# Products accumulated chunk by chunk beside the modulation loads, the modulation spread over heads and merge, and the last FFN weights kept on chip

## The chip, the cores and the metric

One Trainium2 chip; the program runs on all 8 of its cores. Each core does one batch element of the same layer, and the cores exchange nothing. The metric is device time in microseconds (us) of the slowest core. Some executions fall into a slower state: the cores of one die, or of both, show a lower granted TensorE clock than the others, and the time is longer.

## The reference, cut to what matters

```python
cond = jax.nn.silu(c)                                   # c: (8, 2048)
mod = (cond @ w_ada[l] + b_ada[l])[:, None, :]          # 2048 -> 6*2048: shift, scale, gate, twice
sh1, sc1, gt1, sh2, sc2, gt2 = jnp.split(mod, 6, axis=-1)
h = rmsnorm(x, norm1_w[l]) * (1.0 + sc1) + sh1          # x: (8, 2048 tokens, 2048)
x = x + gt1 * hybrid_mixer(h, ...)     # h @ w_in; 8 A heads and 4 B heads; gated merge; @ w_o
h = rmsnorm(x, norm2_w[l]) * (1.0 + sc2) + sh2
x = x + gt2 * swiglu(h, w_ffn_in[l], w_ffn_out[l])      # hidden width 5632
return rmsnorm(x, final_norm_w)
```

All inputs are float32. `w_ada` alone is 96 chunks of 128 output columns, 1 MB each in float32, used once per batch element. The first 32 (shift and scale of the first norm) are needed before the first product of the mixer. The other 64 are needed later: the first gate in the projection, shift and scale of the second norm before the FFN, the second gate in the FFN's output.

## The kernel before: the parts that matter

The kernel works through the 2048 tokens in two halves of 1024. Each half has the stages heads (projections and recurrences of the 12 heads), merge, projection and FFN. Before the first half there is a start stage: load x, compute the norm, form 32 modulation chunks. Every operation goes into a graph. A list scheduler with a rough time model picks, for each engine, the order in which the operations are emitted: among ready operations, the lowest key first. So the order on an engine is fixed when the program is built.

```python
    def schedule(self):                        # (cut)
            for o in cand[e]:
                if o.ready <= bt + 1e-9:
                    k = o.key
                    ...
                    if pk is None or k < pk:
                        pick, pk = o, k
```

Weights come through a ring of slots of 4 KB per partition, by loads that GpSimd (POOL) issues and that cast float32 to bf16. Everything that is loaded with `wload` shares this ring, and loads are issued in one order.

```python
        def wload(src, ncols, key=0.0):
            i = wpos[0] % NSLOT                # NSLOT = 7
            wpos[0] += 1
            t = sb(WOF + i * 4096, ncols, BF16)
            ...
            dma('pool', t, src, wsem[i], writes=[full], nbytes=128 * ncols * 4, key=key - 20.0)
            return t

        def ada_chunk(m, w, cond):             # one modulation chunk: a 2048-column product-sum on VectorE (DVE)
            stt(w, w, 1.0, cond, ALU.mult, ALU.mult, accum=col(modr, m), key=2.0)
```

The start, with a ring of five modulation chunks of its own:

```python
        def phaseA_first():
            adar = ring(172 * KB, 5, 2048, BF16)
            for k in range(16):                # x, in 16 loads of 128 x 1024 float32, from another queue (SP)
                dma('sp', xall[k], xT[k, :, 0:ST], xsem[k], writes=[xall[k]], nbytes=1 << 19, key=-500)
            for i in range(32):
                kc, m = i // 2, (16 if i % 2 == 0 else 0) + i // 2
                w = adar()
                dma('pool', w, w_ada_d[m], asem[i % 5], writes=[w], nbytes=1 << 20, key=-400)
                ada_chunk(m, w, cond0)
                ...                            # squares of x, their sum, the norm
                        for hf in range(2):    # 32 multiplies by the norm, keys 0 to 1.5: ahead of the products' 2.0
                            tt(H(xall[k], hf), H(xall[k], hf), H(rs, hf), ALU.mult, key=0.1 * k)
            for k in range(16):                # then h, on ScalarE (ACT)
                for hf in range(2):
                    act(H(hT[k], hf), H(xall[k], hf), AF.Identity, bias=col(mod, k), scale=col(a1, k), key=0.1 * k)
```

The other 64 chunks, in the first half: two per step of merge, projection and first FFN quarter, through the weight ring.

```python
                dense(w_in_d[72 + fc], hT, ev_mb)      # merge
                if s == 0:
                    ada_some(2, condC)                 # wload + ada_chunk + small columns
            ...
            for fc in range(12):
                proj(fc, (0, 1), wload(w_o_d[fc], 2048))
                if s == 0:
                    ada_some(2, condC)
```

The end of each half normalises and stores in two halves of 512 tokens (`final(0)`, `final(1)`), each 16 tiles.

Of the kernel before, what the change touches and what calls it, by code (L numbers as in the profile page):

```python
# [7 lines left out]
F32 = mybir.dt.float32  # L8
# [11 lines left out]
NSLOT = 7  # L20
# [56 lines left out]
class Graph:  # L77
# [15 lines left out]
    def op(self, eng, fns, reads=(), writes=(), cost=0.2, key=0.0, dsem=None, nbytes=0, table=None):  # L93
# [11 lines left out]
        for t in writes:  # L105
            for k in t.keys:
                w = self.lastw.get(k)
                if w is not None:
                    preds.setdefault(w, 1)
                for r in self.readers.get(k, ()):  # L110
                    preds.setdefault(r, 1)
        preds.pop(o.idx, None)
# [120 lines left out]
def build_nc(trace=None):  # L233
# [21 lines left out]
    with ExitStack() as es:  # L255
# [108 lines left out]
        def act(out, in_, func, bias=None, scale=None, key=0.0):  # L364
# [8 lines left out]
            g.op('act', lambda e: e.activation(out=out.ap, in_=in_.ap, func=func, **kw), reads=[in_] + aps,  # L373
                 writes=[out], cost=cost, key=key, table=TABLE.get(func))

        def tt(out, in0, in1, op, key=0.0, in1ap=None, outap=None, in0ap=None):
# [3 lines left out]
                 reads=[in0, in1], writes=[out], cost=0.155 + in0.ncols * 0.00104, key=key)  # L380

# [7 lines left out]
        def stt(out, in0, s, in1, op0, op1, key=0.0, accum=None):  # L389
# [3 lines left out]
            g.op('dve', lambda e: e.scalar_tensor_tensor(out=out.ap, in0=in0.ap, scalar=v, in1=in1.ap, op0=op0, op1=op1, **kw),  # L393
# [13 lines left out]
        def dma(q, out, in_, sem, reads=(), writes=(), nbytes=0, key=0.0):  # L407
            oa = out.ap if hasattr(out, 'keys') else out
            ia = in_.ap if hasattr(in_, 'keys') else in_
            g.op(q, lambda e: e.dma_start(out=oa, in_=ia), reads=list(reads), writes=list(writes), dsem=sem,  # L410
                 nbytes=nbytes, cost=0.6, key=key)
# [6 lines left out]

        def wload(src, ncols, key=0.0):
            i = wpos[0] % NSLOT  # L420
            wpos[0] += 1
            t = sb(WOF + i * 4096, ncols, BF16)
            full = sb(WOF + i * 4096, 2048, BF16)
            dma('pool', t, src, wsem[i], writes=[full], nbytes=128 * ncols * 4, key=key - 20.0)
            return t

        def H(t, hf):
            return t.cols(hf * 512, hf * 512 + 512)

        def dense_half(w, acts, hf, evac, gk=GK):  # L430

            nk = len(acts)
            p = bank(dbank())
            for k0 in range(0, nk, gk):
# [3 lines left out]
                mm(fns, [w] + [H(acts[k], hf) for k in ks], [p], 0.2154 * len(ks))  # L438
                g.K += 0.2154 * len(ks)
# [9 lines left out]
        osem = [g.newsem("o") for _ in range(16)]  # L449
        csem = [g.newsem("c") for _ in range(10)]  # L450
        cond_f = sb(200 * KB - 8 * KB, 2048, F32)

        def load_cond(dst, tmp, sem):
            dma('sp', tmp, c_d[0:1, :].broadcast_to([128, D]), sem, writes=[tmp], nbytes=1 << 20)
            act(dst, tmp, AF.Silu)

        dma('sp', smalls, smalls_d[:, :], csem[0], writes=[smalls], nbytes=1 << 16)
        cond0 = sb(200 * KB, 2048, BF16)
        load_cond(cond0, cond_f, csem[1])
        for t_, c0, s_ in ((ident, 0, 2), (m64, 128, 3), (m128, 640, 4), (cm64, 1152, 5), (cm128, 1664, 6)):  # L460
            dma('pool', t_, cst_d[:, c0:c0 + t_.ncols], csem[s_], writes=[t_], nbytes=t_.ncols * 512)
# [20 lines left out]
        def ada_chunk(m, w, cond):  # L482
            stt(w, w, 1.0, cond, ALU.mult, ALU.mult, accum=col(modr, m), key=2.0)


        def norm_finish(acc, rs, hf):
            p = bank(sbank())
# [5 lines left out]
        def phaseA_first():  # L493
            adar = ring(172 * KB, 5, 2048, BF16)
            asem = [g.newsem("a") for _ in range(5)]
            xall = [sb(Y + 4 * KB * k, 1024, F32) for k in range(16)]
            acc = sb(MG, 1024, F32)
            rs = sb(MG + 4 * KB, 1024, F32)
            r_q = ring(MG + 8 * KB, 3, 1024, F32)
            for k in range(16):  # L500
                dma('sp', xall[k], xT[k, :, 0:ST], xsem[k], writes=[xall[k]], nbytes=1 << 19, key=-500)
            for i in range(32):
                kc, m = i // 2, (16 if i % 2 == 0 else 0) + i // 2
                w = adar()
                dma('pool', w, w_ada_d[m], asem[i % 5], writes=[w], nbytes=1 << 20, key=-400)
                ada_chunk(m, w, cond0)
                if i % 2 == 0:
                    ts(col(a1, kc), col(modr, m), col(bsc1, kc), sm(SM_N1 + kc), ALU.add, ALU.mult)
                else:
                    tt(col(mod, m), col(modr, m), sm(SM_BADA + m), ALU.add)  # L510
                if i < 16:
                    q = r_q() if i else acc
                    act(q, xall[i], AF.Square, key=-300)
                    if i:
                        tt(acc, acc, q, ALU.add, key=-300)
                if i == 15:
                    for hf in range(2):
                        norm_finish(acc, rs, hf)
                    for k in range(16):
                        for hf in range(2):  # L520
                            tt(H(xall[k], hf), H(xall[k], hf), H(rs, hf), ALU.mult, key=0.1 * k)
            for k in range(16):
                for hf in range(2):
                    act(H(hT[k], hf), H(xall[k], hf), AF.Identity, bias=col(mod, k), scale=col(a1, k), key=0.1 * k)


        def phaseA_next(s, step):
            tok0 = s * ST
            if step < 16:
# [6 lines left out]
                dma('sp', x, xT[k, :, tok0:tok0 + ST], xsem[k % 2], writes=[x], nbytes=1 << 19)  # L536
# [12 lines left out]
            for hf in range(2):  # L549
# [4 lines left out]
                if k < 12:  # L554
                    dma('sp', x, xT[k, :, tok0 + hf * 512: tok0 + hf * 512 + 512], xsem[2 + (k % 2) * 2 + hf], writes=[x], nbytes=1 << 18)
# [55 lines left out]
        def frontA(i, h):  # L611
# [20 lines left out]
            dense(w_in_d[8 + i], hT, ev_f)  # L632
            dense(w_in_d[i], hT, ev_q)
            dense(w_in_d[24 + i], hT, ev_g)

        def gk_low():
            dma('sp', wgk2, wgk2_d[:, :], csem[7], writes=[wgk2], nbytes=1 << 18, key=-30)
            dma('pool', wgkl, wgkl_d[:, :], csem[8], writes=[wgkl], nbytes=1 << 18, key=-30)
# [122 lines left out]
        def ada_some(n, cond):  # L761
            for _ in range(n):
                if ada_todo:
                    m = ada_todo.pop(0)
                    ada_chunk(m, wload(w_ada_d[m], 2048), cond)
                    blk = m // 16
                    tt(col(mod, m), col(modr, m), sm(SM_BADA + m), ALU.add, key=2.0)
                    if blk == 2:
                        ts(col(gt1h, m - 32), col(mod, m), 0.5, None, ALU.mult, ALU.bypass, key=2.0)
                    if blk == 4:  # L770
                        ts(col(a2, m - 64), col(mod, m), 1.0, sm(SM_N2 + m - 64), ALU.add, ALU.mult, key=2.0)

        phaseA_first()
        for s in range(NST):
            tok0 = s * ST

            vt = None
            for i in range(8):
                h = newhead(1)
                frontA(i, h)  # L780
                if i % 4 == 0:
                    vt = vgroup(i // 4)
                tail(h, 64, 128, vt, (i % 4) * 128, persA[i], SM_ANW, [yT[i]])
            gk_low()
            for i in range(4):
# [4 lines left out]
                tail(h, 128, 256, vt, (i % 2) * 256, persB[i], SM_BNW, [yT[8 + 2 * i], yT[9 + 2 * i]])  # L790

# [5 lines left out]
            condC = sb(196 * KB, 2048, BF16)  # L797
            if s == 0:
                load_cond(condC, sb(Z, 2048, F32), csem[0])
                ada_todo += list(range(32, 48)) + list(range(64, 80)) + list(range(48, 64))  # L800
            cst = {}

            def merge_a(fc):
# [17 lines left out]
                if s == 0:  # L821
                    ada_some(2, condC)
# [43 lines left out]
            for fc in range(12):  # L866
# [173 lines left out]
```

## Time and profile before

| | us |
|---|---|
| before, timed executions | 3867.65 and 3868.89 fast; 4132.95 and 4259.19 slow |
| before, profiled execution | 3866.53, fast |
| core 5, the slowest: span | 3865.5 |

The page of the profiled execution, in parts: busy time per engine (PE is TensorE, DVE VectorE, ACT ScalarE, POOL GpSimd), then strips of 40 equal slices in tenths busy, then the chain of work that ended last.

```profile
PE 3623.2 (94%) x17656; PEld 1661.3 (43%) x17656; DVE 1432.2 (37%) x2303; ACT 890.1 (23%) x1252; POOL 358.6 (9%) x683
...
PE   0199999999899999999999999999999999999997
...
DMA  8944446878969644565447334555564454544544
...
PE 90%; DMA 5%; DVE 2%; issue 1%; SPq 1%; ACT 0%; POOL 0%; DVEq 0%; ACTq 0%; POOLq 0%
```

TensorE is on the chain for 90% of the span, and its strip shows where it is not busy: the first two slices (a slice is 97 us), one dip at the eleventh, the end. In all views L393 and the like are lines of the kernel's source, often those of a helper; SB is the on-chip memory, PS the accumulators that matmuls write. The next view gives the busy time of each engine in chosen stretches of core 5. The columns after the bounds are the stretch's length, busy time and number of instructions of PE, PE's weight loads, DVE, ACT and POOL, then the granted TensorE clock, the mean busy share of the 16 DMA engines, and the rate in GB/s.

```profile
core 5: us, PE busy (x) PEld busy (x) DVE busy (x) ACT busy (x) POOL busy (x), PEclk, DMA share, GB/s
0.00:97.00 97.00, 3.66 (x4) 1.18 (x4) 36.43 (x61) 24.99 (x25) 9.84 (x22) 0.93 0.82 174
97.00:197.00 100.00, 17.10 (x49) 6.05 (x50) 83.45 (x105) 23.89 (x32) 14.24 (x27) 0.59 0.89 142
217.00:623.00 406.00, 405.94 (x2351) 195.64 (x2349) 210.39 (x427) 199.96 (x270) 27.44 (x52) 1.00 0.41 68
...
963.00:1178.00 215.00, 188.77 (x829) 82.67 (x828) 126.21 (x179) 58.33 (x83) 26.39 (x50) 0.94 0.84 146
1178.00:2020.00 842.00, 842.00 (x3898) 381.69 (x3897) 219.60 (x303) 112.85 (x168) 77.57 (x147) 1.00 0.57 101
3836.00:3866.00 30.00, 2.96 (x7) 0.69 (x4) 22.14 (x34) 2.48 (x4) 0.00 (x0) 0.60 0.72 269
```

In 1178:2020 PE is never idle: 3898 matmuls in 842 us are 0.216 us each. The Trainium skill ("TensorE: Matmul & The Clock Gate", Part 1) gives 215.7 ns from start to start for a matmul of 512 columns once warm; the trace agrees. So a stage can be judged by how long it takes for its number of matmuls. In the first 197 us there are 48 dense ones. The heads (217:623) have no PE gap, and DVE and DMA are only half and two fifths busy there: that is the room which the change wants to use.

The start in time order. The first line is the DMA strip of 0 to 200 us in slices of 5 us; then come lines of the timeline of DVE, POOL and PE (start, duration, instruction, count, and in brackets the idle time before it and what ended that).

```profile
DMA  3999999999999997200008999999999999999920
```

```profile
82.19 19.35 DVE L377 TENSOR_TENSOR SB<-SB 128x512 f32<-128x512 f32 x32 [4.52 <-ACT SB L373]
101.46 2.28 DVE L393 SCALAR_TENSOR_TENSOR SB<-SB 128x2048 bf16<-128x2048 bf16 x1
...
104.30 0.53 POOL L410 DMA_DIRECT2D SB<-w_ada_l  x1 [93.09 <-DVE SB L393]
...
121.56 5.24 PE L436 MATMUL PS<-SB 128*128 128x512 bf16 x16 [40.84 <-ACT SB L373]
```

The five chunks of the ring fill early. DVE gets to the first one at 101.5 us, after all 32 multiplies. Only then can POOL issue the sixth chunk (104.30, after 93 us), and in the strip the DMA engines stand from about 80 to 105 us. The tail: DVE first runs the 16 outputs of the previous 512 tokens (10.7 us), and only then reaches the last evacuations, the norm and 16 more.

```profile
3833.45 10.69 DVE L393 SCALAR_TENSOR_TENSOR SB<-SB 128x512 f32<-128x512 f32 x16 [0.43 <-ACT SB L373]
...
3848.58 2.04 PE L488 MATMUL PS<-SB 128*128 128x512 f32 x2 [11.67 <-DVE SB L377]
...
3852.14 10.69 DVE L393 SCALAR_TENSOR_TENSOR SB<-SB 128x512 f32<-128x512 f32 x16 [3.71 <-ACT SB L373]
```

### The profile page before, as it was taken

What the parts mean: (1) busy time and instruction counts of PE and PEld (TensorE: products, weight loads), DVE (VectorE), ACT (ScalarE), POOL (GpSimd) and SP (SyncE); (2) the same over time, 40 slices, a digit from 0 to 9 for tenths busy, and PEclk for the clock granted to TensorE, in tenths of its full rate; (3) what the DMA queues carried; (4) which work ended last, traced back from release to release, by engine and by line L of the source; (5) the groups of instructions that cost most, each with busy time, mean ns of one, the idle gap of its engine ahead of it and who ended that gap; (6) DMA issues with size and microseconds to landing.
All of it is one profiled execution on the core that took longest, in us unless ns stands there. A gap on an engine that the chain in (4) does not pass through costs nothing.

```text
span 3865.5 us, 45674 instructions; the slowest of 8 cores (3851.0 to 3865.5 us)
## 1 busy us (share of the span) xinstructions
PE 3623.2 (94%) x17656; PEld 1661.3 (43%) x17656; DVE 1432.2 (37%) x2303; ACT 890.1 (23%) x1252; POOL 358.6 (9%) x683
## 2 busy tenths in 40 slices
PE   0199999999899999999999999999999999999997
PEld 0044444444344444444444444444444444444443
DVE  3845644444653302132145664312143121211116
ACT  2256533111141100030025663311114000000002
POOL 1100000111101100000000000011000000100000
PEclk9599999999899999999999999999999999999998
DMA  8944446878969644565447334555564454544544
GB/s 175 147 71 67 66 67 120 139 128 130 188 107 166 139 77 66 85 137 99 72 71 168 63 58 66 114 77 77 81 126 72 66 86 72 82 77 67 86 68 118
DMA packets 123045, 380.86 MB, mean 99 GB/s; under 512 B 13776, under 2 KB 16720, under 8 KB 122448
## 3 DMA queue, kind: packets, MB, share of 16 engines
q0 software_dynamic: 97776, 315.44, 50.7%
q1 hardware_dynamic: 25056, 62.49, 5.6%
q8 instruction: 145, 2.38, 0.2%
q14 instruction: 68, 0.56, 0.0%
HBM read 676.48 MB, written 16.78 MB: 179 GB/s over the span
## 4 chain that ended last, share of the span: by engine, by line
PE 90%; DMA 5%; DVE 2%; issue 1%; SPq 1%; ACT 0%; POOL 0%; DVEq 0%; ACTq 0%; POOLq 0%
PE PS L436 82%; PE PS L602 5%; DMA SB<-w_ada_l 3%; DVE SB L393 1%; DMA SB<-smalls 1%; SPq L410 1%; DVE SB L377 1%; DMA SB<-w_o_l 1%; DMA SB<-w_in_l 0%; PE PS L712 0%; PE PS L734 0%; PE PS L729 0%; PE PS L651 0%; PE PS L745 0%; DMA SB<-w_fi_l 0%
## 5 line engine op out<-in xcount | busy, mean ns | idle before, releaser
L436 PE MATMUL PS<-SB 128*128 128x512 bf16 x15104 | 3303.4, 381 | 132.3 <-ACT SB L373 105.4
L436 PEld LDWEIGHTS PS<-SB 128*128 128x128 bf16 x15104 | 1477.3, 98 | 1920.9 <-issue 174.7
L373 ACT ACTIVATE SB<-PS 128x512 f32<-128x512 f32 (+1 forms) x580 | 350.2, 614 | 2236.4 <-PE PS L436 2025.1
L377 DVE TENSOR_TENSOR SB<-PS,SB 128x512 bf16<-128x512 f32 x240 | 165.6, 690 | 1041.4 <-PE PS L436 927.5
L373 ACT ACTIVATE SB<-SB 128x512 f32<-128x512 f32 (+5 forms) x504 | 342.4, 713 | 568.3 <-DVE SB L393 276.1
L393 DVE SCALAR_TENSOR_TENSOR SB<-PS,SB 128x512 f32<-128x512 f32 (+1 forms) x400 | 297.0, 747 | 449.0 <-PE PS L436 385.0
L377 DVE TENSOR_TENSOR SB<-SB 128x512 f32<-128x512 f32 (+5 forms) x543 | 333.6, 631 | 220.0 <-ACT SB L373 156.3
L393 DVE SCALAR_TENSOR_TENSOR SB<-SB,PS 128x128 f32<-128x128 f32 (+2 forms) x448 | 206.5, 461 | 406.7 <-PE PS L436 360.7
L393 DVE SCALAR_TENSOR_TENSOR SB<-SB 128x2048 bf16<-128x2048 bf16 (+2 forms) x224 | 307.8, 1398 | 113.5 <-DMA SB<-w_ada_l 92.7
L602 PE MATMUL PS<-SB 128*128 128x512 bf16 x1024 | 232.4, 381 | 6.2 <-DVE SB L401 5.9
L373 ACT ACT_TABLE_LOAD x152 | 195.0, 1283 | 132.2 <-PE PS L436 71.5
L410 POOL DMA_DIRECT2D SB<-w_fi_l x176 | 92.9, 528 | 1018.7 <-PE PS L436 988.3
L602 PEld LDWEIGHTS PS<-SB 128*128 128x128 bf16 x1024 | 98.3, 98 | 120.8 <-issue 9.9
L410 POOL DMA_DIRECT2D SB<-w_in_l x144 | 76.0, 529 | 785.3 <-PE PS L436 421.3
L410 POOL DMA_DIRECT2D SB<-w_fo_l x128 | 67.6, 528 | 637.5 <-PE PS L436 637.5
L488 PE MATMUL PS<-SB 128*128 128x512 f32 x24 | 14.9, 722 | 88.7 <-DVE SB L386 77.1
L410 POOL DMA_DIRECT2D SB<-w_ada_l x96 | 50.8, 530 | 379.3 <-DVE SB L393 158.5
L401 DVE CAST SB<-PS 128x512 bf16<-128x512 f32 x64 | 44.2, 690 | 97.2 <-PE PS L602 97.2
L573 DVE TENSOR_TENSOR_SCAN SB<-SB 128x512 f32<-128x512 bf16 x48 | 58.1, 1218 | 30.1 <-ACT SB L373 30.0
L488 PEld LDWEIGHTS PS<-SB 128*128 128x128 f32 x24 | 4.9, 222 | 92.5 <-issue 91.6
L401 DVE CAST SB<-SB 128x512 bf16<-128x512 f32 x96 | 40.3, 420 | 0.0
L410 POOL DMA_DIRECT2D SB<-w_v_l x32 | 17.0, 544 | 192.6 <-PE PS L436 150.7
(31 smaller groups left out, 373.7 us busy)
## 6 DMA issues: line engine op xcount, KB each, us to landing
SB<-w_fi_l POOLq DMA_DIRECT2D x176, 512.0 KB, 5.2
SB<-w_in_l POOLq DMA_DIRECT2D x144, 512.0 KB, 6.5
SB<-w_ada_l POOLq DMA_DIRECT2D x96, 512.0 KB, 10.1
SB<-w_fo_l POOLq DMA_DIRECT2D x128, 352.0 KB, 4.3
SB<-xT SPq DMA_DIRECT2D x64, 512.0 KB, 12.2
SB<-w_v_l POOLq DMA_DIRECT2D x32, 512.0 KB, 6.2
SB<-w_o_l POOLq DMA_DIRECT2D x32, 512.0 KB, 11.6
outT<-SB SPq DMA_DIRECT2D x64, 256.0 KB, 6.5
```

The lines of the kernel that those rows point to most:

```text
L373: g.op('act', lambda e: e.activation(out=out.ap, in_=in_.ap, func=func, **kw), reads=[in_] + aps, writes=[out], cost=cost, key=key, table= ...
L377: g.op('dve', lambda e: e.tensor_tensor(out=outap if outap is not None else out.ap, in0=in0ap if in0ap is not None else in0.ap, in1=in1ap ...
L393: g.op('dve', lambda e: e.scalar_tensor_tensor(out=out.ap, in0=in0.ap, scalar=v, in1=in1.ap, op0=op0, op1=op1, **kw), reads=[in0, in1] + a ...
L401: g.op('dve', lambda e: e.tensor_copy(out=outap if outap is not None else out.ap, in_=inap if inap is not None else in_.ap), reads=[in_], ...
L410: g.op(q, lambda e: e.dma_start(out=oa, in_=ia), reads=list(reads), writes=list(writes), dsem=sem, nbytes=nbytes, cost=0.6, key=key)
L436: fns = [(lambda e, k=k: e.matmul(p.ap, w.ap[:, k * 128:(k + 1) * 128], H(acts[k], hf).ap, start=(k == 0), stop=(k == nk - 1))) for k in ks]
L488: mm([lambda e: e.matmul(p.ap, onesD.ap, H(acc, hf).ap, start=True, stop=True)], [onesD, H(acc, hf)], [p], 0.9)
L573: g.op('dve', lambda e: e.tensor_tensor_scan(out=dst.ap, data0=mask.ap, data1=src.ap, initial=0.0, op0=ALU.mult, op1=ALU.add), reads=[mask ...
L602: fns = [(lambda e, i=i, j=j, p=p, tb=tb: e.matmul(p.ap, hT[4 * i + j].ap[:, tb * 128:(tb + 1) * 128], ws[i].ap[:, j * 512:(j + 1) * 512], ...
```

## The change

Its intent: let the start's matmuls run while the modulation chunks still come in, put the remaining 64 chunks where DVE and DMA have room, and shorten the end. The diff, cut to its core:

```diff
-NSLOT = 7
+NSLOT = 6
...
-        def phaseA_first():
-            adar = ring(172 * KB, 5, 2048, BF16)
+        def phaseA_first(ws):
+            adar = ring(172 * KB, 8, 2048, BF16)
...
+            for hf in range(2):
+                for k in range(16):                       # x in 32 pieces, first 512 tokens first
+                    x = H(xall[k], hf)
+                    dma('sp', x, xT[k, :, hf * 512:hf * 512 + 512], (xsem, osem[2])[hf][k], writes=[x], nbytes=1 << 18, key=-500)
...                                                         # squares summed on PE instead of DVE
+            banks = [[bank(2 * j + hf) for hf in range(2)] for j in range(4)]
+            hts = []
+            for kc in range(16):
+                for i in range(2):
...
+                    dma('pool', w, w_ada_d[m], asem[n % 8], writes=[w], nbytes=1 << 20, key=-400 + n)
+                    ada_chunk(m, w, -400)
...
+                for hf in range(2):
+                    x = H(xall[kc], hf)
+                    tt(x, x, H(rs, hf), ALU.mult, key=-350)     # now after the products
+                for hf in range(2):
+                    hts.append(act(H(hT[kc], hf), H(xall[kc], hf), AF.Identity, bias=col(mod, kc), scale=col(a1, kc), key=-350))
+                for j in range(4):                              # 4 weights x 2 x 512 tokens = 8 banks
                     for hf in range(2):
+                        p = banks[j][hf]
+                        mm([... ws[j] chunk kc, hT[kc], start=(kc == 0), stop=(kc == 15) ...], key=-100)
...
+        ws = [wload(w_in_d[c_], 2048, key=-380 + 8 * j + 3) for j, c_ in enumerate((8, 0, 24, 9))]
+        banks, hts = phaseA_first(ws)
...
+                if s == 0 and i > 1:
+                    ada_some(3)                           # A heads 2 to 7
...
+                if s == 0:
+                    ada_some(4)                           # B heads
...
-                    ada_some(2, condC)                    # merge keeps 2 per step
+                    ada_some(2)
...
-            for fc in range(12):
+            for fc in range(10):
                 proj(fc, (0, 1), wload(w_o_d[fc], 2048))
-                if s == 0:
-                    ada_some(2, condC)
```

Beside this core, c reaches the 128 partitions through PE instead of by a load of 1 MB; the constants are loaded late; six instead of four products bridge the norm before the FFN; in the last quarter of the FFN all 16 output weights are loaded at once, so that the last 512 tokens can be done as two pieces of 256; and the outputs of `final` get a later key and, for these pieces, stores grouped by four.

## The prediction

> I predict the fast state: the profiled run before took 3866.5 us, the timed runs 3868 to 4259; the slower ones I take for the slow state.
>
> **What bounds it now.** TensorE: the chain of waits is 90% PE. Undisturbed, a dense 128x512 matmul costs 0.216 us (windows, 1178:2020, 3898 matmuls in 842 us). All 17656 at such rates need about 3590 us (estimate), so some 275 us are lost. Matmul counts window by window show where:
> - 0 to 197 us: only 48 dense matmuls (10 us of work); 186 us lost. Timeline: x lands until 73 us; DVE runs 32 normalising multiplies (19 us, ending 101.5) before any modulation product, so the ring of 5 chunks is full and the DMA share falls to 0.1 at 80 to 97. Then 27 chunks come at about 3.2 us each at DMA share 1.0 (11.6 MB in 69 us).
> - 640 to 675 (heads to merge): 9 us, behind a 1 MB broadcast of c.
> - 963 to 1178 (projection and FFN start, first half): 34 us, waits for w_o, w_fi and w_ada, DMA share 1.01, clock 0.82.
> - 2020 to 2072 (between the halves): 8 us.
> - Tail: 28 us from the last dense matmul to the end; DVE first ran 16 outputs of the previous half (10.7 us), then the last evacuations, the norm, and 16 more.
>
> **What the change does, costed.**
> 1. Start. Multiplies now rank after the products, ring 8, constants and c broadcasts leave, four w_in loads join. DMA work: x 8.4 MB at 285 GB/s (hardware queue: 62.5 MB in 5.6% of the span) 30 us; 36 loads at 3.2 us 115; constants 3, two prefetches 6, start-up 3: the last chunk lands near 157 and is used by 164. DVE needs 16 x 5.9 us, so it just hides. By then 128 dense matmuls (27.6 us) are done, against 48 at 197, less 3 us for evacuating eight banks. Gain 47 us. The Trainium skill ("PSUM — Partial Sum Buffer", Specifications) gives eight banks per partition; the start takes them all, so the next products wait for evacuation.
> 2. Modulation: 64 chunks move from merge, projection and FFN into heads and merge. Heads have DMA share 0.42 and DVE at 0.52; 34 chunks of 2.3 us plus small columns add some 90 us of DVE over 440 (to about 0.72) and 0.25 of DMA. Projection then has 16 loads plus x, under the PE's 110 us. Gain 33 + 7, minus 7 us for DVE delays in the heads.
> 3. Six products instead of four hide the norm before the FFN: 1 us.
> 4. Late final outputs at the boundary: 3 us.
> 5. Tail: deferred outputs, last quarter of 256 columns, grouped stores: 28 to about 15 us, less 2 for DVE backlog: 11 us.
> 6. Six weight slots instead of seven: nothing; a slot lasts PE 6.9 us, a load takes 3.2.
>
> Sum about 95 us.
>
> **Prediction: 3770 us, 8 in 10 between 3715 and 3830. Faster by over 2%: 0.69; within 2%: 0.29; slower: 0.02.**
>
> **What would show it.** Windows: dense work steady from 160 to 170 us, DMA share near 1 until then; no PE gap near 640 and in the projection; heads up to 10 us longer, DVE share near 0.7; last matmul to end 13 to 17 us.
>
> **What would make it wrong.** The in-order DVE puts a multiply that waits for the norm ahead of landed chunks, and the DMA idles again (start 185 to 200; time near 3800). The products delay the heads' state chain or hold weight slots and starve PE (20 to 40 us). Or DMA streams overlap better than I add them (3735). Few fast runs.

## The result and the profile after

| | before | after |
|---|---|---|
| fast executions | 3867.65, 3868.89 | 3805.62, 3807.78, 3810.40 |
| slow executions | 4132.95, 4259.19 | 3922.97 (profiled), 4195.23, 4208.56 |
| ratio of fast runs, 95% interval | | 0.9844, 0.9815 to 0.9873: within 2% |

A ratio is the mean time of one kernel's fast runs over the mean of the other's fast runs of the same rounds, so it is not quite the ratio of medians. The output is correct. About 60 us were gained where 95 were predicted; the time lies inside the predicted range, and the class does not match the favoured one.

The profiled execution of the changed kernel was slow, so its cores have to be looked at first. The view of cores:

```profile
core 5: 3801.5 us, clock 0.992
...
die 0 (median of its cores): 3909.1 us, clock 0.958
die 1 (median of its cores): 3792.4 us, clock 0.992
```

Die 1 is undisturbed: its four cores took 3782 to 3805 us, like the cores of the fast executions (3778 to 3810). I therefore read core 5, the same core as before, whose records are complete in both traces. The stretches of core 5 after the change, same columns:

```profile
core 5: us, PE busy (x) PEld busy (x) DVE busy (x) ACT busy (x) POOL busy (x), PEclk, DMA share, GB/s
0.00:97.00 97.00, 46.03 (x46) 12.02 (x46) 25.65 (x50) 18.26 (x29) 10.93 (x24) 1.00 0.98 186
97.00:181.00 84.00, 54.49 (x157) 19.30 (x158) 74.14 (x102) 34.70 (x51) 14.04 (x27) 0.82 0.78 133
181.00:611.00 430.00, 412.79 (x2371) 197.45 (x2369) 303.60 (x579) 221.79 (x292) 47.27 (x90) 0.99 0.68 112
...
954.00:1066.00 112.00, 112.00 (x517) 50.62 (x516) 52.28 (x77) 32.76 (x50) 8.44 (x16) 1.00 0.58 111
1066.00:1981.00 915.00, 915.00 (x4232) 414.67 (x4231) 230.34 (x323) 139.58 (x206) 79.15 (x150) 1.00 0.53 93
3786.00:3802.00 16.00, 0.67 (x2) 0.30 (x2) 7.75 (x19) 2.36 (x6) 2.12 (x3) 0.66 0.39 132
```

The projection (954:1066) and the FFN (1066:1981) are now without a PE gap. The heads (181:611) take 430 us for the work that took 406, and 17 us of PE idling are new there; the other 7 us are in PE's own busy time (413 against 406 us, at a granted clock of 0.99 against 1.00). DVE's 304 us of 430 are 0.71 of the stretch, as predicted.

For a table by stage I count dense 128x512 matmuls along the trace. A stage ends when the first matmul of the next one starts: the first head products, made in the start after the change, are the first 128; the heads end after 1792, merge after 3328, projection after 3840, FFN after 8064.

| stage of core 5, us | before | after | change | predicted |
|---|---|---|---|---|
| start, up to 128 dense matmuls | 216.7 | 180.6 | -36.1 | -47 |
| heads, first half | 406.6 | 430.7 | +24.1 | +7 |
| merge, first half | 346.4 | 342.7 | -3.7 | -7 |
| projection and FFN, first half | 1062.0 | 1026.8 | -35.2 | -34 |
| heads, second half, with the boundary | 444.1 | 441.7 | -2.4 | -3 |
| merge and projection, second half | 446.9 | 446.9 | 0 | 0 |
| FFN, second half, and tail | 942.9 | 932.1 | -10.8 | -11 |
| sum | 3865.5 | 3801.5 | -64.1 | -95 |

(The rows are rounded, so that a sum can be off in its last digit.) The shortfall of 31 us is in the first three rows: 11 in the start, 17 in the heads, 3 in the merge. The rest is as predicted.

The start after the change: first the DMA strip of 0 to 200 us, then DVE.

```profile
DMA  4999999999999999998875525999999995927999
```

```profile
48.99 2.29 DVE L398 SCALAR_TENSOR_TENSOR SB<-SB 128x2048 bf16<-128x2048 bf16 x1 [1.75 <-DMA SB<-w_ada_l]
...
51.40 0.16 DVE L378 TENSOR_TENSOR SB<-SB 128x1 f32<-128x1 f32 x1
94.68 3.10 DVE L378 TENSOR_TENSOR SB<-SB 128x512 f32<-128x512 f32 x5 [43.13 <-ACT SB L374]
```

And POOL, which issues the loads, then PE at the end of the start:

```profile
51.83 0.53 POOL L415 DMA_DIRECT2D SB<-w_ada_l  x1 [3.91 <-DVE SB L378]
100.53 0.53 POOL L415 DMA_DIRECT2D SB<-w_ada_l  x1 [48.17 <-DVE SB L398]
```

```profile
180.56 13.97 PE L449 MATMUL PS<-SB 128*128 128x512 bf16 x64 [0.83 <-ACT SB L374]
```

DVE has done eight products by 51.4 us. The next thing in its order is a multiply by the norm, and it waits for that for 43 us, until ACT has the norm of the first 512 tokens at 94.7. Meanwhile the eight buffers of the ring fill up again, and POOL issues nothing from 51.83 to 100.53. In the strip the DMA engines stay nearly full until about 100 us, because x is still coming in (its last packet landed at 104 us by the trace's DMA records), and then there is a hole: the slices from 100 to 125 us show 7, 5, 5, 2 and 5 tenths, and over these 25 us the mean DMA share is 0.54, so some 12 us of DMA time are empty. From 94.7 on DVE works through 24 products and 32 multiplies until 176.5. Its waits between 95 and 177 us (total us, times, longest; the first wait of 43 us, which ends at 94.7, is counted in):

```profile
DVE SB L378 <- ACT SB L374: 48.0, 2, 43.1
```

So there is one more pause of 4.9 us, for ACT, and none for a modulation chunk: the chain of waits runs through x and the norm of the second 512 tokens to 116.6 us, and from there through DVE's own work to the end of the start. The hole in the DMA strip is not on it.

In the heads, POOL's issues between 286 and 325 us, and PE a little later:

```profile
298.96 0.53 POOL L415 DMA_DIRECT2D SB<-w_ada_l  x1 [3.70 <-DVE SB L398]
303.80 0.53 POOL L415 DMA_DIRECT2D SB<-w_ada_l  x1 [4.32 <-DVE SB L398]
...
322.88 0.53 POOL L415 DMA_DIRECT2D SB<-w_ada_l  x1 [3.01 <-PE PS L632]
323.75 0.53 POOL L415 DMA_DIRECT2D SB<-w_in_l  x1 [0.34 <-issue]
```

```profile
333.90 3.32 PE L449 MATMUL PS<-SB 128*128 128x512 bf16 x8 [2.93 <-DMA SB<-w_in_l]
```

Eight modulation loads in a row are issued between 286.85 and 322.88, five of them after a wait for DVE to finish with the slot's previous chunk. The `w_in` load behind them is issued at once when its turn comes (its own wait is none, "issue"): it had waited only for the loads ahead of it. It lands 10.0 us later, and PE has been idle for 2.9 us by then. The Trainium skill ("DMA: Bandwidth & Descriptors", Anatomy of one DMA) states that a semaphore wait of a load is served on the issuing sequencer, before the load is dispatched; this is what these lines look like. PE's waits on core 5, from 181 to 960 us (total us, times, longest):

```profile
PE PS L449 <- DMA SB<-w_in_l: 8.6, 5, 2.9
PE PS L728 <- DVE SB L398: 4.0, 3, 1.8
PE PS L762 <- DVE SB L406: 2.4, 1, 2.4
PE PS L449 <- DMA SB<-w_upa_l: 2.1, 1, 2.1
```

So there are two sorts of wait: for weights, and for DVE in the heads' state chain (L728 and L762 are its small matmuls). The sizes differ between cores: on core 7, whose heads took 422.9 us, the waits for `w_in` are 0.9 us. After the start, where the prediction charged 3 us for emptying the eight banks, PE's only wait up to 194 us is the 0.83 us for ACT in the line at 180.56.

The tail after the change, by the timeline:

```profile
3789.87 0.67 PE L506 MATMUL PS<-SB 128*128 128x256 f32 x2 [3.96 <-DVE SB L378]
...
3791.64 6.42 DVE L398 SCALAR_TENSOR_TENSOR SB<-SB 128x256 f32<-128x256 f32 x16 [1.91 <-ACT SB L374]
```

The last dense matmul ends at 3785.9, 15.6 us before the end; 13 to 17 had been predicted. No outputs of an earlier piece stand ahead of the last norm any more. No run undoes the boundary, the tail or the six products alone; that they gained what they were meant to is read from the stages only.

### The profile page after: what moved, and what is told of

It reads as the page before. It is cut to its first block, busy times and chain, and to the rows that moved or that the text cites. A ratio compares the mean times of both kernels' runs of the same rounds, so it can differ in the third digit from the quotient of the medians.

```text
span 3921.8 us, 46040 instructions; the slowest of 8 cores (3781.8 to 3921.8 us)
## 1 busy us (share of the span) xinstructions
PE 3776.9 (96%) x17555; PEld 1723.3 (44%) x17902; DVE 1404.3 (36%) x2310; ACT 893.2 (23%) x1287; POOL 379.7 (10%) x709
## 4 chain that ended last, share of the span: by engine, by line
PE 89%; DMA 4%; DVE 2%; SPq 2%; issue 2%; ACT 0%; POOL 0%; DVEq 0%; POOLq 0%; ACTq 0%
PE PS L449 81%; PE PS L632 5%; DVE SB L398 2%; SPq L415 2%; DMA SB<-w_in_l 2%; DMA SB<-w_ada_l 1%; DMA SB<-xT 1%; DMA SB<-w_v_l 1%; PE PS L745 0%; DMA outT<-SB 0%; PE PS L762 0%; PE PS L767 0%; PE PS L778 0%; ACT SB L374 0%; PE PS L506 0%
## 5 line engine op out<-in xcount | busy, mean ns | idle before, releaser
L449 PE MATMUL PS<-SB 128*128 128x512 bf16 (+1 forms) x14837 | 3357.6, 387 | 35.4 <-DMA SB<-w_in_l 12.8
L449 PEld LDWEIGHTS PS<-SB 128*128 128x128 bf16 x15152 | 1508.5, 100 | 1849.8 <-issue 409.4
L374 ACT ACTIVATE SB<-PS 128x512 f32<-128x512 f32 (+2 forms) x585 | 352.1, 613 | 2348.5 <-PE PS L449 2101.9
L398 DVE SCALAR_TENSOR_TENSOR SB<-PS,SB 128x512 f32<-128x512 f32 (+2 forms) x416 | 300.1, 727 | 488.2 <-PE PS L449 438.5
L378 DVE TENSOR_TENSOR SB<-SB 128x512 f32<-128x512 f32 (+6 forms) x517 | 307.5, 610 | 228.5 <-ACT SB L374 161.4
L398 DVE SCALAR_TENSOR_TENSOR SB<-SB 128x2048 bf16<-128x2048 bf16 (+3 forms) x240 | 312.4, 1324 | 72.6 <-DMA SB<-w_ada_l 60.1
L632 PE MATMUL PS<-SB 128*128 128x512 bf16 x996 | 229.1, 381 | 9.0 <-ACT SB L374 6.0
L632 PEld LDWEIGHTS PS<-SB 128*128 128x128 bf16 x1024 | 98.3, 98 | 122.2 <-issue 10.8
L526 PE MATMUL PS<-SB 128*128 128x512 f32 x64 | 52.5, 941 | 45.1 <-ACT SB L374 45.1
L551 PE MATMUL PS<-SB 128*128 128x512 bf16 x125 | 41.5, 488 | 30.5 <-ACT SB L374 30.2
L526 PEld LDWEIGHTS PS<-SB 128*128 128x128 f32 x64 | 14.9, 270 | 81.2 <-issue 80.8
```

Source lines behind the costliest of these rows:

```text
L374: return g.op('act', lambda e: e.activation(out=out.ap, in_=in_.ap, func=func, **kw), reads=[in_] + aps, writes=[out], cost=cost, key=key, ...
L378: g.op('dve', lambda e: e.tensor_tensor(out=outap if outap is not None else out.ap, in0=in0ap if in0ap is not None else in0.ap, in1=in1ap ...
L398: return g.op('dve', lambda e: e.scalar_tensor_tensor(out=out.ap, in0=in0.ap, scalar=v, in1=in1.ap, op0=op0, op1=op1, **kw), reads=[in0, i ...
L449: fns = [(lambda e, k=k: e.matmul(p.ap, w.ap[:, k * 128:(k + 1) * 128], H(acts[k], hf).ap, start=(k == 0), stop=(k == nk - 1))) for k in ks]
L526: mm([lambda e, k=k, hf=hf, q=q: e.matmul(nb[hf].ap, onesD.ap, q.ap, start=(k == 0), stop=(k == 15))], [onesD, q], [nb[hf]], 0.87, key=-300)
L551: mm([lambda e, p=p, j=j, hf=hf: e.matmul(p.ap, ws[j].ap[:, kc * 128:(kc + 1) * 128], H(hT[kc], hf).ap, start=(kc == 0), stop=(kc == 15)) ...
```

## The experiments

Two losses had to be explained. For the start: theory A, DVE's order is at fault (a multiply that waits for the norm stands ahead of landed chunks); theory B, the norm is late because x shares the DMA engines with the weight loads. For the heads: theory C, the products' time on DVE delays the state chain; its rival, the loads of the modulation chunks hold slots of the weight ring and turns of its queue. Twelve kernels were run, each edit made to the changed kernel. Each was timed against the kernel before in the same rounds. Fast runs of the kernel before differ by 0.6% over the chips used (3856 to 3878), so small differences between kernels are read from stages, on cores with complete records, and from the ratios.

### e_order: every multiply tied behind a product that is already in

```diff
-                    tt(x, x, H(rs, hf), ALU.mult, key=-350)
+                late = prods[min(29, 15 + kc)]
+                    tt(x, x, H(rs, hf), ALU.mult, key=-405, after=[late])
```

> One edit to the changed kernel: in the start, the two normalising multiplies of input chunk k are tied behind modulation product 15+k, so the in-order DVE no longer stands for the norm (it stood from 51.4 to 94.7 us) with landed modulation chunks unread. Theory A (DVE order): modulation loads go on while x lands; DMA share stays near 1 and the last first-product matmul group ends near 160 us instead of 177 to 180; total 12 to 20 us less than the changed kernel, ratio to before about 0.980. Rival B (the start is bound by the sum of DMA work, or by x arriving late, whatever the DVE order): x only lands later by what the modulation loads take, and the start still ends at 175 to 185; ratio stays 0.984. The heads should keep their 16 to 23 us of PE gaps in both.

Measured: correct; fast runs 3821.2 and 3824.2. The start took 194 to 198 us on its complete cores, some 16 more than the changed kernel's 179 to 181; both expectations had it at 185 or earlier, so neither was met. DVE on core 5:

```profile
94.32 0.69 DVE L378 TENSOR_TENSOR SB<-SB 128x512 f32<-128x512 f32 x1 [0.17 <-DVE SB L398]
132.36 0.76 DVE L378 TENSOR_TENSOR SB<-SB 128x512 f32<-128x512 f32 x2 [37.34 <-ACT SB L374]
```

DVE no longer stood at 51 us, it stood from 95 to 132. With products running on, the ring was refilled all the time and x came in still later: its last packet landed at 124 us, and the norm of the second 512 tokens was known only at 132. Theory A falls as a cause of its own: a better order of DVE alone moves the stop, because the lateness of x depends on how many weight loads run beside it. My count of the trace's DMA packet records between 15 and 90 us shows how the two queues share the engines (records of 4 bytes left out):

```
kernel    window     weight loads (cast)        x
e_order   15-90 us   2422 packets, 381 ns each  2422 packets, 124 ns each
changed   15-90 us   2244 packets, 396 ns each  2544 packets, 131 ns each
e_xfirst   5-28 us   -                          3299 packets, 111 ns each
```

The Trainium skill ("DMA: Bandwidth & Descriptors", Queues, rings and completion order) says that each DMA engine takes turns between the queues that have work, packet by packet. The equal counts of e_order agree with it. Since a packet of a casting load took three times as long as one of x, x gets a quarter of the time.

### e_xfirst: weight loads wait until 28 of the 32 pieces of x have landed

```diff
+                    xl = dma('sp', x, xT[k, :, hf * 512:hf * 512 + 512], ...)
+                    if hf == 1 and k == 11:
+                        xlate = [xl]
-                    dma('pool', w, w_ada_d[m], asem[n % 8], ..., key=-400 + n)
+                    dma('pool', w, w_ada_d[m], asem[n % 8], ..., key=-400 + n, after=xlate)
```

(and the same `after` on the four `w_in` loads)

> The other way to the same end: all modulation and weight loads of the start are held until 28 of the 32 pieces of x have landed, so that the norm is known before any product. Theory A: x lands by 30 to 40 us, the norm by 45 to 50, and from then on DVE never stands; DMA work of 36 loads at 3.2 us follows, so the start ends at 155 to 168 us. Rival B (one queue alone does not fill the DMA engines): x alone takes over 45 us at a DMA share well under 1, and the start ends at 170 us or later. Heads unchanged.

Measured: correct; fast runs 3786.0 twice, ratio 0.9806 (0.9778 to 0.9835). The start took 157.0 to 163.6 us; the heads stayed at 424 to 430. The DMA strip of 0 to 200 us, and DVE's first multiplies:

```profile
DMA  3999998999999999999999999999998899750004
```

```profile
31.32 8.52 DVE L378 TENSOR_TENSOR SB<-SB 128x512 f32<-128x512 f32 x14 [11.25 <-ACT SB L374]
```

x lands by 33 us (last packet) instead of 104, the multiplies begin at 31.3 instead of 94.7, and the DMA engines have no hole before 165. This confirms theory B of the list above: with x first, the same order of DVE does no harm. (The expectation uses the letters otherwise: its theory A came true, its rival B, one queue alone not filling the engines, did not.) From 31.5 to 157 us DVE now waits for chunks, which it never did after the norm in the changed kernel; so here the DMA engines set the pace:

```profile
DVE SB L398 <- DMA SB<-w_ada_l: 20.1, 21, 6.6
```

It shortens the start by 16 to 24 us, core against core. The next stage begins where the predicted sum of DMA work (the last chunk near 157, used by 164) had put it.

### e_xwide: x in 16 pieces with rows of 4 KB instead of 2 KB

```diff
-            for hf in range(2):
-                for k in range(16):
-                    x = H(xall[k], hf)
-                    dma('sp', x, xT[k, :, hf * 512:hf * 512 + 512], ...)
+            for k in range(16):
+                dma('sp', xall[k], xT[k, :, 0:ST], xsem[k], writes=[xall[k]], nbytes=1 << 19, key=-500)
```

> The start loads x in 16 whole pieces with rows of 4 KB, as the kernel before does, instead of 32 halves with rows of 2 KB; nothing else of the changed kernel is edited. In the trace of the changed kernel the two DMA queues alternate packet for packet (2544 packets of x of 2048 bytes at 131 ns against 2244 of the weights of 4096 bytes at 396 ns between 15 and 90 us), which leaves x 28% of the engines; before, with 4096-byte packets of 229 ns, x had 45%. Theory P (packet alternation: the halved rows are why x lands at 97 us): x lands by 70 to 80 us, the norm follows by 85, and the first products end at 163 to 170 us instead of 177 to 180; ratio to before about 0.981. Rival Q (x is late because of the number of weight loads queued, in bytes): x still lands at 90 us or later and the start ends at 175 or later.

Measured: correct; fast runs 3801.4 to 3804.1, ratio 0.9839 (0.9804 to 0.9875). The packets now had the same size in both queues and again alternated (1444 casting ones at 390 ns, 1443 of x at 228 ns between 15 and 70 us), and x's share rose from 28% to 37%. The last of x landed at 89 us instead of 104. But the norm of the first 512 tokens was not known earlier (95.8 against 94.7), since wide pieces bring both halves at the same pace, and the start took 173 to 181.5. That is a gain of about 2 us on the mean of the complete cores; the expected 163 to 170 was missed. Wider rows alone, in this order, bring x in 15 us sooner but not the norm; without the loads beside it (e_xfirst) x is in by 33 us.

### e_noada: the 64 chunks neither loaded nor multiplied (wrong)

```diff
-        ada_todo += list(range(32, 48)) + list(range(64, 80)) + list(range(48, 64)) + list(range(80, 96))
+        memset(mod.cols(32, 96), 0.25)
+        memset(gt1h, 0.125)
+        memset(a2, 1.25)
```

> Wrong result on purpose: the 64 modulation chunks of heads and merge are neither loaded nor multiplied (their columns are set to constants). It measures what they cost now. If they are what the heads of the first half lose against those of the second, the PE gaps in heads and merge vanish: first-half heads plus merge shorten by 15 to 25 us on the slower cores (5 and 6 in the profile of the change), all cores then agree within 5 us, ratio to before about 0.979. If the loss has another cause (cold start of the pipeline, eight banks taken), they keep their length and the ratio stays 0.984.

Measured: relative error 0.37; fast runs 3773.7 and 3788.8, ratio 0.9794 (0.9747 to 0.9840). The heads took 407 to 409 us with no PE gap over 1.3 us, the merge 335.3. (Two cores took 423 in the heads, also without a gap, at a granted clock of 0.92 from 180 to 400 us.) So the heads' whole loss of about 24 us, and up to 7 in the merge, come from the modulation work put there.

### e_short: the same loads, products of 256 columns instead of 2048 (wrong)

```diff
-                    ada_chunk(m, wload(w_ada_d[m], 2048), 4.0)
+                    ada_chunk(m, wload(w_ada_d[m], 2048).cols(0, 256), 4.0, cond.cols(0, 256))
```

> Wrong result on purpose: the modulation products of heads and merge read 256 of 2048 columns, so DVE spends about 0.5 us instead of 2.3 us on each, while every load stays. Theory C (DVE time: products delay the heads' state chain, and hold weight slots so that the in-order load queue waits for them): PE gaps in heads and merge fall to a few us, nearly as without modulation, ratio about 0.979 to 0.981. Rival D (DMA work and contention of the 64 loads): gaps on weight loads stay at about 12 us of the 23, ratio 0.983 to 0.984.

Measured: relative error 0.24; fast runs 3804.9 to 3805.6, ratio 0.9856 (0.9833 to 0.9878). The heads took 427.6 to 435.1 us, the merge 336.5 to 344.7: no relief. The waits for weights stayed; on core 7 in this run:

```profile
PE PS L449 <- DMA SB<-w_in_l: 11.9, 5, 5.3
```

Theory C falls: in the heads of core 5 DVE was busy for 243 us instead of 304, and nothing was gained. (The edit changes costs in the scheduler's model, so the order moved too: on core 5 the load queue has another kind of load in 26 of the 104 places of the heads. c_best, below, shows the same from the other side: DVE as busy as ever, and no loss.)

### e_thin: 128 of 2048 columns loaded and multiplied, in the same slots as in e_short (wrong)

```diff
+                    ada_chunk(m, wload(w_ada_d[m, :, 0:128], 128), 4.0, cond.cols(0, 128))
```

> Wrong result on purpose: each of the 64 chunks loads 128 of its 2048 columns and multiplies these alone; slots, order of the load queue and number of instructions stay as in the run with short products. Against that run it takes away the bytes only. Theory D (bytes): heads fall from 427 to 435 us to about 410, merge to 335. Theory S (slots and queue order): they stay within 6 us of the run with short products.

Measured: relative error 0.25; fast runs 3782.8 and 3783.3. The heads took 414.3 to 419.8 us, the merge 335.3 to 336.5. About half to two thirds of the loss is gone. Against what the expectation says, the run does not take away the bytes alone: in core 5's trace the load queue has another kind of load than e_short's in 23 of the 106 places of the heads. So that the bytes are a large part is likely, not shown; and 8 to 13 us remain although almost nothing is loaded or multiplied.

### e_own: modulation chunks in buffers of their own

```diff
+        def aload(m, ring_):                  # 4 buffers in the A heads, 2 in the B heads, 2 in the merge
+            off, s_ = ring_[apos[0] % len(ring_)]
+            apos[0] += 1
+            t = sb(off, 2048, BF16)
+            dma('pool', t, w_ada_d[m], asems[s_], writes=[t], nbytes=1 << 20, key=-20.0)
+            return t
-                    ada_chunk(m, wload(w_ada_d[m], 2048), 4.0)
+                    ada_chunk(m, aload(m, ring_), 4.0)
```

> The 64 modulation chunks of heads and merge get buffers of their own (4 in the heads of mixer A, 2 in those of B, 2 in the merge) instead of slots of the six-slot weight ring; bytes, DVE work and the one in-order load queue stay. Theory S (slots: a chunk waiting for its product holds a weight slot, and the queue behind it): heads plus merge of the first half lose at most 8 us against the run without modulation (407 + 335), instead of 15 to 31; ratio about 0.981. Theory D (the bytes: 64 more loads on the DMA engines make weights land late): heads stay at 422 to 432 us and the ratio at 0.984.

Measured: correct; fast runs 3796.5 to 3798.1, ratio 0.9826 (0.9791 to 0.9862). The heads took 410.0 to 412.0 us and the merge 335.3 to 339.4: nearly the whole loss is gone, with all bytes and all products still there. But the start took 191 to 194 us, because the heads' chunks found their buffers free: on core 5 ten of them were issued before the start's end, and DVE ran eight of their products (2.3 us each) there. How much of the delay is due to the loads and how much to the products, the run does not separate.

### e_own2: the same, with these loads held until the last piece of h is made

```diff
+            dma('pool', t, w_ada_d[m], asems[s_], writes=[t], nbytes=1 << 20, key=-20.0, after=hts[31:])
```

> The run with buffers of their own, mended: there the load queue took 4 of the heads' chunks into the start (start 191 to 196 us, which hid the gain); here these loads wait for the end of the start. Expected: start back at 177 to 181 us, heads 409 to 414 instead of 423 to 432, merge 335 to 339, total some 18 to 22 us under the changed kernel, ratio to before 0.979. If the heads' gain came only from the 4 chunks taken early, the heads are at 420 or more.

Measured: correct; fast runs 3778.9 to 3781.7, ratio 0.9797 (0.9778 to 0.9816). Start 175 to 178, heads 410.0 to 415.5, merge 335.3 to 337.7. On core 6 between 181 and 960 us the only wait of PE for a weight is

```profile
PE PS L632 <- DMA SB<-w_v_l: 0.5, 1, 0.5
```

and on the other complete cores such waits are 1.2 us at most. Putting the chunks through the weight ring is thus what cost the time in the heads. One reservation: taking the chunks out of the ring also gives the weights more slots and makes the scheduler order the one load queue anew (the longest row of chunk loads in the heads is five instead of eight). The run does not separate held slots from waiting turns, nor either from the new order, and no run has seven slots with the chunks in the ring.

### e_back: the modulation back in merge, projection and FFN

```diff
-                if s == 0 and i > 1:
-                    ada_some(3)
-                if s == 0:
-                    ada_some(4)
+                if s == 0:
+                    ada_some(2)               # in each of ten projection steps
+                    if s == 0 and q == 0:
+                        ada_some(2)           # in the first FFN quarter
```

> Undo of one part: no modulation in the heads; the 64 chunks are taken two at a time in merge, projection and the FFN's first quarter, as before, without the broadcasts of c. It prices the spreading: heads 407 us as without modulation; merge 338 to 345, projection 112 to 130 instead of 111.6, FFN 915 to 922. If the projection stays near 112, the broadcasts and the 1024-column-wide backlog were the old loss there and not the number of chunks, and the total falls to about 3785, under the changed kernel; if it goes back to 130, the total is about 3800, the same as the changed kernel.

Measured: correct; fast runs 3820.6 to 3827.5, ratio 0.9895 (0.9865 to 0.9926). The heads are back at 407 to 408 us, the projection took 135.6 to 142.4 and the FFN 920.7 to 926.4. Projection and total came out above the expected 112 to 130 and 3800. Against the changed kernel's 3806 to 3810 the spreading is worth about 15 us net (20 by the ratios): some 35 gained behind, some 20 lost in the heads.

### e_noacc: no products beside the start's loads

```diff
-                for j in range(4):
-                    for hf in range(2):
-                        p = banks[j][hf]
-                        mm([...])
-        ws = [wload(w_in_d[c_], 2048, key=-380 + 8 * j + 3) for j, c_ in enumerate((8, 0, 24, 9))]
+        ws = []
```

(the first heads' products are then ordinary ones, their weights are loaded late in the start)

> Undo of one part: the start keeps its modulation loop but multiplies nothing on TensorE beside it, and its four weight loads are not made there; the first products follow after the start, as before. It prices the accumulation. Four loads of 3.2 us less beside x: the norm comes some 12 us sooner, and since DVE is busy without a gap from the norm on, the last input chunk is ready at 160 to 168 us instead of 175 to 178. But 128 matmuls, 27.6 us at full clock, then lie after it. Net: 10 to 18 us slower than the changed kernel, ratio to before 0.987 to 0.989. If the accumulation pays in full, 24 us or more slower.

Measured: correct; fast runs 3807.8, 3809.7, 3833.6, 3838.0, ratio 0.9907 (0.9845 to 0.9969). The two higher runs include the profiled one, in which cores 0 and 1 had a clock of 0.84 to 0.85 between 180 and 400 us; the two lower ones are level with the changed kernel. DVE on core 5:

```profile
80.89 3.10 DVE L378 TENSOR_TENSOR SB<-SB 128x512 f32<-128x512 f32 x5 [36.43 <-ACT SB L374]
```

The norm is known 14 us earlier (80.9 against 94.7), because four weight loads fewer share the engines with x. The 128th dense matmul was reached at 183.4 us against 180.6. So in the changed kernel the accumulation by itself, the change's main idea, yields about 3 us: the four weights it needs early delay x by nearly as much as the accumulation saves. I had expected 10 to 18 us more for this run; that was wrong.

### c_best: e_xfirst and e_own2 together

The edit is the sum of the two.

> Both mends together: x first (start 157 to 163 us), own buffers for the modulation chunks that wait for the end of the start (heads 409 to 414, merge 335 to 339). If the two losses are separate, the gains add: span 3755 to 3765 us in the fast state, ratio to before 0.971 to 0.974, so over 2% faster than the kernel before and 1.1% faster than the changed kernel. If the start's mend only moves DMA work into the heads, the heads grow back by some 8 us and the ratio is 0.976.

Measured: correct; five fast runs, 3761.2 to 3763.3; ratio 0.9751 (0.9732 to 0.9771), faster than the kernel before by over 2%. Core 5, DMA strip of 0 to 200 us and stretches:

```profile
DMA  3999998999999999999999999999997899999999
```

```profile
...
97.00:158.00 61.00, 30.79 (x74) 9.23 (x74) 41.94 (x52) 16.61 (x23) 9.72 (x19) 0.58 1.00 163
158.00:566.00 408.00, 408.00 (x2372) 197.20 (x2371) 307.87 (x588) 207.81 (x281) 49.93 (x95) 1.00 0.74 123
```

The start took 155.5 to 163.0 us, the heads 407.5 to 409.8, the merge 335.3 to 337.9. In the heads DVE is as busy as in the changed kernel (308 us against 304) and DMA more (0.74 against 0.68), and PE has no gap: neither engine was too full. The start is now limited by the DMA engines, which are busy throughout. The total is as expected, the ratio just above the expected 0.971 to 0.974. The two repairs add up: 15 and 18 us by the ratios (0.9844 less 0.9806 and 0.9797, times 3860), 36 together. Against the changed kernel this is about 1%, measured by way of the kernel before and not side by side.

### c_noacc: c_best without the accumulation

> The mended kernel (x first, own buffers) without the products beside the modulation loads: prices the accumulation where the norm no longer waits on weight loads. If it pays only when x is out of its way, the 128th dense matmul, which the mended kernel reaches at 156 to 163 us, comes at 166 to 174 us here, and the total is 8 to 14 us longer than the mended kernel's 3762, ratio to before 0.977 to 0.979. If the accumulation is worth nothing here either, as it was in the changed kernel (180.6 against 183.4 us on core 5), the ratio stays at 0.975 to 0.976.

Measured: correct; fast runs 3775.4 to 3777.0, ratio 0.9783 (0.9759 to 0.9806). The 128th dense matmul was reached at 171.6 to 179.4 us, 16 later than in c_best. With x first, the accumulation is worth 12 us by the ratios and 16 by the stage, within the 10 to 18 us that I had expected in e_noacc; in the changed kernel it was hidden behind the late norm.

## Why the prediction was right or wrong

Right, within 2 us: projection and FFN of the first half (-35.2 against -34), the boundary between the halves (-2.4 against -3), the tail (-10.8 against -11), and that six slots would do for the stages without modulation (the second half's merge and projection did not change). Part of the closeness is luck: of the 35 us in projection and FFN, e_back puts back 30 on core 5, where 33 were predicted for the moved chunks, and the other 5, for which 1 was predicted, are left to the six products and the missing broadcast (not tested alone). DVE's share of the heads, 0.71, was right too.

Wrong by 11 us: the start. The step that failed is in point 1: "the last chunk lands near 157 and is used by 164. DVE needs 16 x 5.9 us, so it just hides." The sum of DMA work was right: c_best and e_xfirst, which keep the engines busy, reach the next stage at 156 to 164. What failed is the overlap: DVE's work was to run beside the loads from early on. I added x at 285 GB/s as if it came first; in truth it got about 28% of the engines' time, its last packet landed at 104 us, and the first norm was known at 94.7. DVE had then stood 43 us for the norm, and 24 products and 32 multiplies still lay ahead of it: 76 us of work in the 82 us up to 176.5, with one pause of 4.9 us, for the norm of the second 512 tokens, and none for a chunk. So DVE, started late, ended the start, and not the loads; the 12 us of DMA time that stayed empty between 100 and 125 follow from buffers that DVE had not yet freed. With x first it is the other way round: DVE waits 20 us for chunks (e_xfirst). My own warning named half of it, that "the in-order DVE puts a multiply that waits for the norm ahead of landed chunks". e_order shows that curing only this half makes the start longer; e_xfirst shows that x first cures it. Before the change this lateness did less harm, as the ring of five chunks stopped by itself and left the engines to x, which had landed by about 73 us.

Wrong by 17 us: the heads, "minus 7 us for DVE delays in the heads", which measured 24. I costed the chunks in time of DVE and share of DMA, both rightly, and set the term by DVE. e_short and c_best show that DVE's time is not the cause, e_own and e_own2 that with buffers of their own the same chunks cost 3 to 9 us instead of 16 to 26 (against the 406.6 before), in c_best 1 to 3. The cost came from putting the chunks through the ring: six slots, filled by one queue in order, in which 34 chunks that nobody needs soon stood ahead of weights that PE needed at once (with the reservation at e_own2). The warning "or hold weight slots and starve PE (20 to 40 us)" was the right one, and I gave it too little weight; point 6, that six slots instead of seven cost nothing, is shown only for stages where no chunk sat in them; whether a seventh would have helped in the heads, no run shows.

Wrong by 3 us: the merge, 3.7 instead of 7 gained; e_noada and c_best give another 7 on core 5 (335.3 and 335.7), so it is the same cause.

Left open: how the heads' 24 us divide between weight loads issued late (12 us on core 5, under 2 on core 7) and a DVE that stands at a chunk not yet landed and delays the state chain; e_thin, which takes the bytes away (and changes the order) and half of the loss with them, would fit both, and the own buffers of e_own2 remedy both.

## What to carry to other kernels

A load that everything waits for, such as x before a norm, should have the DMA engines to itself: sum up not only how much has to be moved but in which order it lands. Work that fills idle engines is better given buffers of its own: through the ring of the critical loads it took their slots or turns, and the idle shares that made room for it said nothing of that. An engine that had to stand early can be the limit of a stage though it is busy from then on: look at when its work begins, and not only at how much it is. And when a change overlaps two things, check that what the overlap needs early does not delay what both wait for: here four early weights cost nearly all that the accumulation gained.

## What the Trainium skill lacked or had wrong

- "DMA: Bandwidth & Descriptors", Queues, rings and completion order, has the turn-taking by packet, and the runs agree (2422 packets against 2422). It lacks the consequence: the queues share the engines by the time of their packets. A casting packet took 381 to 410 ns and one of x 124 to 131 (2 KB) or 228 (4 KB), so x got 25 to 37%.
- The same page, Bandwidth, gives about 358 GB/s per core as what the HBM side allows. It has no rate for a casting load. In e_xfirst, with the DMA share at 1.0, x alone came at 345 GB/s at best (25 to 30 us; 294 on the mean of 5 to 28 us), and casting loads alone at 173 GB/s written (60 to 120 us), which is 346 of float32 read: as if a casting load counts by its float32 bytes.
- The same page, Anatomy of one DMA, gives a fit of 2.0 us + bytes / 436e3 per load, so 3.2 us for the 512 KB written or 4.4 for the 1 MB read (estimates by that fit). The shortest landing of a modulation chunk that I found in the changed kernel's start was 5.0 us, with all eight cores loading, and up to 53 us with a full queue ahead of it. The fit is low for this case; the page's table of measured loads has 6.15 us for 1 MB, so 5.0 lies between its two figures.
- "TensorE: Matmul & The Clock Gate", Part 1, has a limiter that takes a whole die to 13/16 of the clock once three of its cores run dense matmuls, and holds it while the load lasts. The profiled slow execution agrees in part: all four cores of die 0 were granted 0.8125 for 670 to 754 us of it. But the four cores of die 1 beside them, and all eight of the profile before, ran such work too and were never granted 0.8125 (1.00 for 3608 us or more). The page does not say why it comes in some executions only, in which a die's mean clock fell from 0.99 to 0.96 or 0.89 and the time rose from 3806 to 3923 or 4200 us.
